# RWKV-7 stage of a hybrid trunk layer: score products that alternate heads, low-rank products on all 128 rows, small sums moved beside recurrence products

## The chip, the cores and the metric

The kernel runs on 1 core of one Trainium2 chip. The metric is the device time of one execution in microseconds (us). Before the change it is 2905.15 us, the median of 3 runs (2900.6 to 2907.33).

## What is computed

One layer of a streaming encoder over 4096 tokens of 1024 features: four mixers of 256 columns each (RWKV-7, pooling, mLSTM, retention), a gated embedding and an output projection with a layer norm. The change lies in the RWKV-7 mixer alone. Cut to what matters, with 4 heads of 64:

```python
z = z + (prev - z) * mu                       # token shift
r, k, v, wl, al = split(z)
decay = exp(-exp(-softplus(-(w0 + tanh(wl) @ w2)) - 0.5))   # low-rank, 64 inner columns
a = sigmoid(a0 + al @ a2)                                    # low-rank, 64 inner columns
kk = heads(k * k_k); kk = kk / max(norm(kk), 1e-12)
k = heads(k) * (1 + (a - 1) * k_a)
def step(state, ...):
    sa = state @ (-kk)
    state = state * w + sa * (kk * a) + v * k
    return state, state @ r
y = head_norm(scan(step)) * ln_w + ln_b + sum(r * k * r_k) * v
```

## The kernel before

The four mixers run one after another, and the output projection last. The RWKV stage (`_rwkv_out`) takes the tokens in 16 blocks of 256. The scan is done in chunks of 64 tokens: the scores of a chunk give a triangular matrix that is inverted, and a recurrence of four chunks carries the state through a block.

What a block goes through is cut into generators ("stages"), and the string `ORDER` says how they interleave. Each word is a stage, a lag in blocks and, after a slash, how many steps of it to run. `C` is one step of the recurrence `chain` of the block before last; there are 12 of them in a pass: per chunk `ry` (state and score products), `sa` (the inverse times the result), and `ds` with the second half of `ry` (state update and output). Between them stand dense projections (`la`, `k`, `r`, `g`, `v`, six products of 128x256 per step of one contraction tile, three for `la`) and small stages:

- `l`: the two low-rank products. Weights `LW` hold an upper and a lower part on 64 rows each. For both products and both column halves there is one matmul of `lah` over 128 rows, and one of `lal` (the lower part of the input) over the 64 rows that hold it.
- `n` and `bn`: sums over a head, 8 products of two columns each, with 64 output rows (128 contraction rows).
- `s0`, `s1`: transposes of `BK` into `st`, scaled into `ST` by VectorE. `p0`, `p1`: the scores of a pair of chunks, `gp`: for head `hh` of a pair (64 contraction rows each) four products, then four VectorE operations that scale and mask them into `g1`. `gp` has one PSUM buffer per head; `l`, `n`, `vt`, `st`, `gp` and `bn` share a pool of two.
- `inv`, `iv`, `pt`, `px`, `pu`, `py`: the inverse `X`, in part on VectorE (`iv`), through DRAM, and in 32-row products; `pt`, `px`, `pu`, `py` run one pass later. `sa` of the next pass reads `X`.

All these products go through `mm` (L273), which keeps them in the program's order on TensorE, so that the string is TensorE's order. The other engines' orders come from the tile scheduler. `soon()` raises the priority of the recurrence's and the inverse's operations there. float32 products are two records each in the trace.

```python
        mm = lambda *args, **kw: keep(nc.tensor.matmul(*args, **kw))
...
                    for p, hh, hv in heads:
                        mm(sa[bs, p, hv], X[bs, 4 * cc + 2 * hh + p], R[bs, p, hv], start=True, stop=True)
                    A.copy(out=SAV[cc][bs, e], in_=sa[bs].rearrange("p a v -> p (a v)"))
...
            for e in range(2):
                V.tensor_copy(out=X[top(e), :, 32:64], in_=t[top(e)])
            yield 0.6
```

Of the kernel before, what the change touches and what calls it, by code (L numbers as in the profile page):

```python
# [9 lines left out]
F32 = mybir.dt.float32  # L10
# [19 lines left out]
ORDER = "C la.0 C k.0/2 C k.0 C r.0/2 C l.0 r.0/3 C r.0/2 n.0 r.0/2 C vt.1 r.0 m.0 C g.0/4 C g.0 v.0/2 C s0.0 v.0/1 pt.1 C p0.0/1 v.0/1 px.1 C p0.0 v.0/2 bn.0 v.0 pu.1 s1.0 p1.0/1 py.1 p1.0 inv.0 iv.0"  # L30
# [12 lines left out]
class Trunk:  # L43
# [27 lines left out]
    def fetch(self, hi, lo, src, nm, eng):  # L71
        """load float32 data and split it exactly into hi + lo"""
# [14 lines left out]
    def weights(self, name, g0, w=G, pool=None, bufs=5, gates=False):  # L87
        """hi and lo parts of columns g0..g0+w of a weight matrix"""
# [16 lines left out]
    def lazy(self, *args, **kw):  # L105
        """a weight group that is loaded where it is first used"""
        box = []
        def get(split=False):
            if not box:
                w, parts = self.weights(*args, **kw)  # L110
                box.append(w)
                if split:
                    return parts
                list(parts)
            return box[0]
        return get

    def load_x(self, b, more=None, between=None):
        """the block's tokens in quarters of the contraction; three of eight come from the pool more"""
# [19 lines left out]
    def dense(self, jobs, nk=KT, apart=False):  # L139
        """out = lhsT.T @ rhs for each job; operands are (hi, lo) by contraction tile.  # L140
        The jobs share one bank unless apart and advance together, so one start flag clears it."""
# [7 lines left out]
    def dense_k(self, jobs):  # L149
        """the same in steps of one contraction tile, in this order on the engine"""  # L150
# [8 lines left out]
    def cols(self, z, w, x, n=2):  # L159
        """columns of one weight group on the partitions, tokens along the row"""  # L160
# [3 lines left out]
    def toks(self, jobs, nk=KT, apart=False):  # L164
        """tokens on the partitions: jobs of (out, weights, x, first token)"""
# [4 lines left out]
    def silu_gate(self, sg, z):  # L170
        """twice z * sigmoid(z)"""
# [13 lines left out]
    # ------------------------------------------------------------------ RWKV  # L185
# [6 lines left out]
    def _rwkv_out(self, es):  # L192
# [20 lines left out]
        # low-rank weights: decay rows (hi, lo), rate rows (lo, hi), against twice the upper part of their input  # L213
# [43 lines left out]
        def mixed(b, out, z, c0, n):  # L257
            """z + (previous token's z - z) * mu, by columns"""
# [11 lines left out]
        # what a block goes through, in pieces: generators that yield the time of the products they have issued  # L270
# [53 lines left out]
        def l(b):  # L324
            # low-rank decay and rate
            la = bl[b]["la"]
            lah = p1.tile([P, 2, TB], F32R, name=f"lah{b}", tag="E")
            lal = p1.tile([P, TB], F32R, name=f"lal{b}", tag="ta")
            lz = [wk.tile([P, 2, TB], F32, name=f"l{g}{b}", tag="wk") for g in range(2)]
            for g in range(2):  # L330
# [3 lines left out]
                V.tensor_tensor(out=lal[own], in0=la[own], in1=lah[own, g].bitcast(F32), op=ALU.subtract)  # L334
                for p in range(2):
                    mm(lz[g][:, p], LW[g][:, p], lah[:, g], start=(p == 0), stop=False, skip_group_check=True)
                    mm(lz[g][:, p], LW[g][own, p], lal[own], start=False, stop=True, skip_group_check=True)
# [20 lines left out]
        def n(b):  # L358
            # squared norm of the removal key, by tokens in the order of the rows of its products
# [11 lines left out]
            # rows (kappa, beta) of an even chunk, (beta, kappa) of an odd one  # L371
# [61 lines left out]
        def s_(b, cc):  # L433
            # token-major copies of (kappa, beta)
# [11 lines left out]
        def p_(b, cc):  # L446
            # scores of the chunk
            BK, rc, AR, g1 = (bl[b][x] for x in ("BK", "rc", "AR", "g1"))
            gp = [wk.tile([P, 2, 2, P], F32, name=f"gp{b}_{cc}_{hh}", tag="wk") for hh in range(2)]
            for hh in range(2):  # L450
                sl = slice(64 * hh, 64 * hh + 64)
                for p in range(2):
                    for e in range(2):
                        mm(gp[hh][:, p, e], BK[sl, p, cc, 2 * e:2 * e + 2].rearrange("p a t -> p (a t)"),
                           AR[cc][sl, p, 2 * e:2 * e + 2].rearrange("p a t -> p (a t)"), start=True, stop=True)
                for p in range(2):
# [5 lines left out]
                yield 0.87  # L462
# [37 lines left out]
        # inverse of I - N, N strictly upper in this layout  # L500
# [23 lines left out]
        def iv(b):  # L524
# [3 lines left out]
            with self.soon():  # L528
                # the four blocks of 4 on the diagonal, row by row from below
# [7 lines left out]
                # pairs of blocks: X12 = X11 (N12 X22), the inner product where N has zeros  # L537
# [25 lines left out]
        def pt(b):  # L563
            # pairs of 16 to blocks of 32: rows and columns of one block of 32, what N has in the pairs meets zeros
# [29 lines left out]
        def pu(b):  # L594
            # blocks of 32 to 64
# [23 lines left out]
        def chain(b):  # L619
            """the four chunks of a block, one after another; yields where their products wait"""  # L620
# [90 lines left out]
    def head_norm(self, pool, Y, eps, nm):  # L711
        """normalise each 64-wide head of Y [P, 2, 256] in place"""
# [18 lines left out]
    # ------------------------------------------------------------------ pooling  # L731
    def pooling(self, es):
# [12 lines left out]
        # the first products wait for these alone  # L745
# [79 lines left out]
    # ------------------------------------------------------------------ retention  # L825
# [133 lines left out]
    # ------------------------------------------------------------------ mLSTM  # L959
    def gates(self, cp, es0):  # L960
        """the stabiliser and the decays of every chunk of 128 tokens, rows (chunk, head)"""
# [69 lines left out]
    def _mlstm(self, es):  # L1031
# [12 lines left out]
        def operand(n):  # L1044
            """the right operand n of v, o and the gate; three of them leave room for a left operand each"""
# [19 lines left out]
        def dense(b):  # L1065
# [31 lines left out]
            # the halves of the block's tokens: rows of the contraction k0 .. k0 + 3, tokens of half c  # L1097
# [68 lines left out]
        def mix(b):  # L1166
# [25 lines left out]
            for c in range(2):  # L1192
# [4 lines left out]
                # decayed scores, transposed: rows are the keys  # L1197
# [22 lines left out]
                # carry of the memory  # L1220
# [16 lines left out]
                # h = num / max(|den|, exp(-m))  # L1237
# [448 lines left out]
```

## Time and profile before

| | before |
|---|---|
| median of 3 runs | 2905.15 us |
| profiled execution: span from first to last instruction | 2898.2 us |
| median less that span (what lies around it, and scatter) | 6.95 us |
| TensorE (PE) busy | 2773.1 us, 96% |
| VectorE (DVE) busy | 2270.0 us, 78% |
| ScalarE (ACT), GpSimd (POOL) busy | 34%, 40% |
| mean granted TensorE clock | 0.974 |

The profile gives no time of the profiled execution other than its span, so that the runs' median stands beside it. PE busy counts a matmul from its start to its end, and matmuls overlap: a stretch that is busy throughout may hold products that follow each other closely or slowly. What a group of products costs is therefore read from the start of its first product to the start of what comes next. The RWKV stage lies between about 1255 and 2190 us of the span.

### The profile page before, as it was taken

Reading aid. Unit: us, or ns where it says so; the run is one execution under the profiler, and the core shown is the slowest. Engines: PE = TensorE matmul, PEld = TensorE weight load, DVE = VectorE, ACT = ScalarE, POOL = GpSimd, SP = SyncE. Lnnn points to the kernel's source line nnn. Section 1 sums busy time; section 2 is a strip of 40 time slices with the busy share of each in tenths; the row PEclk is TensorE's granted clock in tenths of the full one; section 3 lists DMA queues with packets and bytes.
Section 4 is the critical chain, followed back from the end, with each engine's and each line's share of the span. In section 5 each row is a group of like instructions: output and inputs, shape, how many; then the busy total and the mean of one; then the engine's idle time right before and its main releaser. Section 6 shows DMA issues by size and latency. Waiting matters only on the chain.

```text
span 2898.2 us, 57364 instructions
## 1 busy us (share of the span) xinstructions
PE 2773.1 (96%) x21940; PEld 2466.1 (85%) x21940; DVE 2270.0 (78%) x5639; ACT 974.5 (34%) x2100; POOL 1156.9 (40%) x1231
## 2 busy tenths in 40 slices
PE   7899999999999999798999999999999999999997
PEld 7898888878999999688999999998998788777885
DVE  5657788887999999976777777778847566689997
ACT  3423223234433333333333333334423233432221
POOL 6654555553333333421232333223326111156665
PEclk9899999999999999888999999999999999999998
DMA  7743222223211111321111111112437444643441
GB/s 241 218 142 102 59 66 66 63 72 110 71 59 56 59 53 55 103 59 29 47 34 41 44 37 45 34 45 60 133 106 260 149 139 138 221 153 139 148 157 66
DMA packets 250499, 281.13 MB, mean 97 GB/s; under 512 B 69488, under 2 KB 166512, under 8 KB 250224
## 3 DMA queue, kind: packets, MB, share of 16 engines
q1 hardware_dynamic: 250224, 277.46, 30.5%
q8 instruction: 172, 2.82, 0.4%
q14 instruction: 103, 0.84, 0.1%
HBM read 209.69 MB, written 67.70 MB: 96 GB/s over the span
## 4 chain that ended last, share of the span: by engine, by line
PE 41%; DVE 10%; POOL 3%; DMA 2%; issue 2%; ACT 1%; SPq 0%; POOLq 0%; DVEq 0%; ACTq 0%
PE ry L273 3%; PE gp L273 2%; DVE ro L1578 2%; DVE ro L1557 1%; PE sa L273 1%; PE l L273 1%; PE zg L154 1%; DVE ro L1560 1%; PE zpl L147 1%; PE zpl L145 1%; PE zpl L146 1%; PE zg L155 1%; PE zg L156 1%; POOL ro L1561 1%; PE zpe L145 1%
## 5 line engine op out<-in xcount | busy, mean ns | idle before, releaser
L1336 ACT CAST Ah<-xr 128x512 fp32r<-128x512 f32 x189 | 117.0, 620 | 277.7 <-PE zrb L1372 58.7
L1337 DVE TENSOR_TENSOR Al<-xr,Ah 128x512 fp32r<-128x512 f32 x135 | 99.8, 739 | 76.5 <-ACT Ah L1336 75.7
L677 POOL TENSOR_TENSOR SAV<-SAV,bon 64x256 f32<-64x256 f32 x64 | 40.7, 636 | 283.9 <-PE ry L273 282.3
L85 DVE TENSOR_TENSOR xl<-rawx,xh 128x512 fp32r<-128x512 f32 x148 | 120.9, 821 | 39.8 <-ACT xh L84 38.9
L145 PE MATMUL zqk<-xh,wh_w_ml 128*128 128x256 f32 x512 | 149.1, 291 | 1.1 <-ACT xh L1078 1.1
L146 PE MATMUL zqk<-xl,wh_w_ml 128*128 128x256 f32 x512 | 149.1, 291 | 0.3 <-DVE xl L1079 0.3
L147 PE MATMUL zqk<-xh,wl_w_ml 128*128 128x256 f32 x512 | 149.2, 291 | 0.0
L84 ACT CAST xh<-rawx 128x512 fp32r<-128x512 f32 x148 | 91.6, 619 | 168.8 <-DMA rawx<-in_xT 72.3
L1337 POOL TENSOR_TENSOR Al<-xr,Ah 128x512 fp32r<-128x512 f32 x54 | 71.8, 1330 | 135.7 <-ACT Ah L1336 72.2
L1561 POOL TENSOR_TENSOR ro<-ro,ln_b 128x512 f32<-128x512 f32 x64 | 100.6, 1591 | 53.9 <-DVE ro L1560 53.9
L660 DVE SCALAR_TENSOR_TENSOR S<-ds,eC,Se 64x64 f32<-64x64 f32 x256 | 72.5, 283 | 53.4 <-PE ds L273 48.7
L866 POOL TENSOR_TENSOR rot<-rot,sw 128x256 f32<-128x256 f32 x64 | 69.4, 1085 | 94.2 <-DVE sw L865 88.5
L145 PEld LDWEIGHTS zqk<-xh,wh_w_ml 128*128 128x128 f32 x512 | 98.0, 191 | 3.6 <-ACT xh L1078 1.6
L147 PEld LDWEIGHTS zqk<-xh,wl_w_ml 128*128 128x128 f32 x512 | 98.1, 192 | 2.4
L146 PEld LDWEIGHTS zqk<-xl,wh_w_ml 128*128 128x128 f32 x512 | 98.2, 192 | 2.0 <-DVE xl L1079 0.8
L459 DVE SCALAR_TENSOR_TENSOR g<-gp,rc,c_rmask 128x128 f32<-128x128 f32 x256 | 72.1, 343 | 33.9 <-PE gp L273 32.8
L145 PE MATMUL zu<-xh,wh_w_pl 128*128 128x256 f32 x256 | 78.7, 308 | 14.7 <-ACT xh L84 8.9
L1356 POOL TENSOR_TENSOR xr<-xr,xr 128x512 f32<-128x512 f32 x27 | 35.5, 1316 | 141.8 <-DVE xr L1353 141.7
L146 PE MATMUL zu<-xl,wh_w_pl 128*128 128x256 f32 x256 | 78.2, 305 | 12.0 <-DVE xl L85 12.0
L1185 DVE SCALAR_TENSOR_TENSOR xc<-zc,c_convw,xc 128x256 f32<-128x256 f32 x192 | 86.2, 497 | 0.4
L273 PE MATMUL ry<-SAV,g 64*64 64x64 f32 (+1 forms) x1024 | 83.5, 223 | 0.0
L798 DVE SCALAR_TENSOR_TENSOR dp<-s,c_pinv,us 64x256 f32<-64x256 f32 (+1 forms) x64 | 44.5, 695 | 47.9 <-POOL s L784 41.7
(1120 smaller groups left out, 10675.9 us busy)
## 6 DMA issues: line engine op xcount, KB each, us to landing
rawx<-in_xT SPq DMA_DIRECT2D x148, 256.0 KB, 3.3
xr<-in_xT SPq DMA_DIRECT2D x108, 256.0 KB, 2.9
mr<-in_xT SPq DMA_DIRECT2D x64, 256.0 KB, 3.1
rp<-in_x SPq DMA_DIRECT2D x64, 256.0 KB, 3.1
s<-rp SPq DMA_DIRECT2D x64, 256.0 KB, 2.5
yo<-y SPq DMA_DIRECT2D x16, 1024.0 KB, 4.9
ro<-s SPq DMA_DIRECT2D x16, 1024.0 KB, 5.0
out<-ro SPq DMA_DIRECT2D x32, 512.0 KB, 2.6
```

The costliest lines, as they stand in the source:

```text
L84: nc.scalar.copy(out=hi, in_=raw)
L85: eng.tensor_tensor(out=lo, in0=raw, in1=hi.bitcast(F32), op=ALU.subtract)
L145: nc.tensor.matmul(out, lh(k), rh(k), start=(k == 0 and (apart or i == 0)), stop=False, skip_group_check=True)
L146: nc.tensor.matmul(out, lh(k), rl(k), start=False, stop=False, skip_group_check=True)
L147: nc.tensor.matmul(out, ll(k), rh(k), start=False, stop=(k == nk - 1), skip_group_check=True)
L273: mm = lambda *args, **kw: keep(nc.tensor.matmul(*args, **kw))
L459: V.scalar_tensor_tensor(out=g1[cc][:, hh, p, e], in0=gp[hh][:, p, e], scalar=rc[:, cc, e, i:i + 1], in1=msk[:, 64 * e:64 * e + P], op0=AL ...
L660: V.scalar_tensor_tensor(out=Sn[hv, p, hv], in0=ds[hv, p], scalar=eC[hv, p, c:c + 1], in1=Se[hv, p], op0=ALU.mult, op1=ALU.add)
L1185: V.scalar_tensor_tensor(out=xc[:, t], in0=zc[t // 2][:, t % 2, j:j + TB], scalar=cw[:, t, j:j + 1], in1=xc[:, t], op0=ALU.mult, op1=ALU.add)
L1336: self.nc.scalar.copy(out=hi, in_=src)
L1337: eng.tensor_tensor(out=lo, in0=src, in1=hi.bitcast(F32), op=ALU.subtract)
L1561: Q.tensor_tensor(out=rg, in0=rg, in1=ln["ln_b", g], op=ALU.add)
```

## The change

`ORDER` is written anew, the score products alternate the two heads, and the low-rank products all span 128 rows. The input's lower part `lal` gets a second copy with zeros in the other 64 rows (two GpSimd memsets per block). Docstrings and comments are emptied, which moves line numbers by up to 4; they are left out here.

```diff
-ORDER = "C la.0 C k.0/2 C k.0 C r.0/2 C l.0 r.0/3 C r.0/2 n.0 r.0/2 C vt.1 r.0 m.0 C g.0/4 C g.0 v.0/2 C s0.0 v.0/1 pt.1 C p0.0/1 v.0/1 px.1 C p0.0 v.0/2 bn.0 v.0 pu.1 s1.0 p1.0/1 py.1 p1.0 inv.0 iv.0"
+ORDER = "C la.0 C k.0/2 C k.0 C r.0/2 C l.0 r.0/3 C n.0 r.0/4 C vt.1 r.0 m.0 C g.0/4 C g.0 v.0/2 C s0.0 v.0/1 pt.1 C p0.0 v.0/2 px.1 C bn.0 v.0/1 s1.0 v.0/2 pu.1 v.0/1 p1.0 v.0 py.1 inv.0 iv.0"
...
-            lal = p1.tile([P, TB], F32R, name=f"lal{b}", tag="ta")
+            lal = p1.tile([P, 2, TB], F32R, name=f"lal{b}", tag="ta")
...
                 A.copy(out=lah[other, g], in_=la[own])
-                V.tensor_tensor(out=lal[own], in0=la[own], in1=lah[own, g].bitcast(F32), op=ALU.subtract)
+                Q.memset(lal[other, g].bitcast(F32), 0.0)
+                V.tensor_tensor(out=lal[own, g], in0=la[own], in1=lah[own, g].bitcast(F32), op=ALU.subtract)
+            for g in range(2):
                 for p in range(2):
                     mm(lz[g][:, p], LW[g][:, p], lah[:, g], start=(p == 0), stop=False, skip_group_check=True)
-                    mm(lz[g][:, p], LW[g][own, p], lal[own], start=False, stop=True, skip_group_check=True)
+                for p in range(2):
+                    mm(lz[g][:, p], LW[g][:, p], lal[:, g], start=False, stop=(p == 1), skip_group_check=True)
...
             gp = [wk.tile([P, 2, 2, P], F32, name=f"gp{b}_{cc}_{hh}", tag="wk") for hh in range(2)]
-            for hh in range(2):
-                sl = slice(64 * hh, 64 * hh + 64)
-                for p in range(2):
-                    for e in range(2):
+            for p in range(2):
+                for e in range(2):
+                    for hh in range(2):
+                        sl = slice(64 * hh, 64 * hh + 64)
                         mm(gp[hh][:, p, e], BK[sl, p, cc, 2 * e:2 * e + 2].rearrange("p a t -> p (a t)"),
                            AR[cc][sl, p, 2 * e:2 * e + 2].rearrange("p a t -> p (a t)"), start=True, stop=True)
+            for hh in range(2):
                 for p in range(2):
                     for e in range(2):
...
-                yield 0.87
+            yield 0.87
```

The order of instructions changes with it. Three places, all in the pass of block 7.

TensorE, from the inverse's product `px` on, before (`ds`, `ry`: recurrence; `gp_0_1`: scores of the second head; `z7v`: dense projection):

```order
L273 MATMUL px_19636<-X_19135,TD 32x16 x32
L273 MATMUL ds_3_19673<-SAV_1_18693,ST_1_17986 64x64 x4
L273 MATMUL ry_3_19557<-SAV_1_18693,g_1_17988 64x64 x4
L273 MATMUL gp_0_1_19621<-AR_0_19449,BK_19448 128x128 x4
L154 MATMUL z7v<-xh_4_19161,wh_w_rw_14376 128x256
```

The same place now:

```order
L273 MATMUL px_19666<-X_19149,TD 32x16 x32
L273 MATMUL ds_3_19703<-SAV_1_18707,ST_1_17998 64x64 x4
L273 MATMUL ry_3_19573<-SAV_1_18707,g_1_18000 64x64 x4
L273 MATMUL bn_19755<-rkw,rk_19479 64x2 x8
L154 MATMUL z7v<-xh_4_19175,wh_w_rw_14376 128x256
```

The sums `bn` follow the recurrence's products directly, and the second head's scores have gone up to the first head's. `n` is moved in the same way behind the second `ds` and `ry` of the pass.

VectorE, at the end of the pass, before (`g_1`: masked scores of the second pair of chunks; `X<-py`: the last part of the inverse; `v`, `Y`: other work):

```order
L459 SCALAR_TENSOR_TENSOR g_1_19468<-gp_1_0_19803,rc_14302,c_rmask 128x128 x4
L265 SCALAR_TENSOR_TENSOR v_19768<-z7v,c_prm,v_19768 128x255
L268 TENSOR_TENSOR v_19768<-v_19768,zf_19172 128x2
L726 TENSOR_TENSOR Y_19138<-Y_19138,rsr_19712 128x512
L617 COPY X_19135<-py_19813 32x8x32 x2
L459 SCALAR_TENSOR_TENSOR g_1_19468<-gp_1_1_19804,rc_14302,c_rmask 128x128 x4
```

The same place now:

```order
L463 SCALAR_TENSOR_TENSOR g_1_19484<-gp_1_0_19819,rc_14302,c_rmask 128x128 x4
L463 SCALAR_TENSOR_TENSOR g_1_19484<-gp_1_1_19820,rc_14302,c_rmask 128x128 x2
L265 SCALAR_TENSOR_TENSOR v_19790<-z7v,c_prm,v_19790 128x255
L268 TENSOR_TENSOR v_19790<-v_19790,zf_19186 128x2
L463 SCALAR_TENSOR_TENSOR g_1_19484<-gp_1_1_19820,rc_14302,c_rmask 128x128
L730 TENSOR_TENSOR Y_19152<-Y_19152,rsr_19742 128x512
L463 SCALAR_TENSOR_TENSOR g_1_19484<-gp_1_1_19820,rc_14302,c_rmask 128x128
L621 COPY X_19149<-py_19837 32x8x32 x2
```

The second head's four operations, which stood behind the copies into `X`, now stand ahead of them.

VectorE, in the middle of the pass, before (`Z_0`: transpose of `X` as it comes from DRAM; `S`: the recurrence's state; `BK`, `AR`: operands of the scores):

```order
L265 SCALAR_TENSOR_TENSOR r_19416<-z7r,c_prm,r_19416 128x255
L268 TENSOR_TENSOR r_19416<-r_19416,zf_19172 128x2
L402 TENSOR_TENSOR BK_19448<-ta_19332,tw_19331 128x2x128 x2
L408 TENSOR_TENSOR AR_0_19449<-r_19416,E_19340 128x2x2x64
L660 SCALAR_TENSOR_TENSOR S_14298<-ds_2_19500,eC_17864,Se_2_19505 64x64 x4
L567 STREAM_TRANSPOSE Z_0_19578<-X_19135 128x512
```

The same place now:

```order
L265 SCALAR_TENSOR_TENSOR r_19432<-z7r,c_prm,r_19432 128x255
L268 TENSOR_TENSOR r_19432<-r_19432,zf_19186 128x2
L571 STREAM_TRANSPOSE Z_0_19594<-X_19149 128x512
L405 TENSOR_TENSOR BK_19464<-ta_19348,tw_19347 128x2x128 x2
L411 TENSOR_TENSOR AR_0_19465<-r_19432,E_19356 128x2x2x64
L664 SCALAR_TENSOR_TENSOR S_14298<-ds_2_19516,eC_17876,Se_2_19521 64x64 x4
```

The transpose, which waits for a transfer, stands ahead of the operands and of the state update.

## Rows read from the trace of the kernel before

**Rows 1.** Busy time in a 55 us stretch of the RWKV stage, columns as named.

```profile
core 0: us, PE busy (x) PEld busy (x) DVE busy (x) ACT busy (x) POOL busy (x), PEclk, DMA share, GB/s
1475.00:1530.00 55.00, 55.00 (x677) 50.29 (x675) 41.93 (x131) 20.19 (x51) 17.88 (x27) 1.00 0.14 39
```

**Rows 2.** Timeline, PE: start, length, instruction. The low-rank products' first, and what follows.

```profile
1511.07 0.38 PE L273 MATMUL l<-lah,LW 128*128 128x256 f32 x1
...
1513.57 0.39 PE L154 MATMUL z5r<-xh,wh_w_rw 128*128 128x256 f32 x1
```

**Rows 3.** Timeline, PE: dense products before and behind the sums n.

```profile
1518.06 0.28 PE L155 MATMUL z5r<-xl,wh_w_rw 128*128 128x256 f32 x1
1518.18 0.28 PE L156 MATMUL z5r<-xh,wl_w_rw 128*128 128x256 f32 x1
1518.39 0.65 PE L273 MATMUL n<-ones,sq 128*64 128x2 f32 x16
1518.97 0.38 PE L154 MATMUL z5r<-xh,wh_w_rw 128*128 128x256 f32 x1
1519.20 0.28 PE L155 MATMUL z5r<-xl,wh_w_rw 128*128 128x256 f32 x1
```

**Rows 4.** Timeline, PE: scores to the next pass's sa, dense products left out.

```profile
1534.14 1.16 PE L273 MATMUL gp<-AR,BK 64*128 64x128 f32 x8
...
1536.13 0.73 PE L273 MATMUL px<-X,TD 32*32 32x16 f32 x64
1536.79 0.45 PE L273 MATMUL ds<-SAV,ST 128*64 128x64 f32 x8
...
1537.64 1.16 PE L273 MATMUL gp<-AR,BK 64*128 64x128 f32 x8
...
1544.85 0.69 PE L273 MATMUL py<-X,T 32*32 32x32 f32 x32
1545.47 1.16 PE L273 MATMUL gp<-AR,BK 64*128 64x128 f32 x8
1546.55 0.71 PE L273 MATMUL ry<-S,AR 128*128 128x128 f32 x4
...
1550.87 0.68 PE L273 MATMUL sa<-R,X 64*64 64x64 f32 x8
```

**Rows 5.** Timeline, PE: the retention stage's scores, whose heads alternate, and the next product.

```profile
504.91 0.71 PE L920 MATMUL sc<-qT,kT 64*128 64x128 f32 x8
505.56 0.50 PE L1372 MATMUL zrb<-rB6wlg,Ah 128*128 128x512 f32 x1
```

**Rows 6.** Single records' lengths in ns (min/median/max), by line: scores and sums.

```profile
L273 PE MATMUL gp<-AR,BK x512: 272/272/578, 1280.7 to 2062.8; 64*128 64x128 f32 x171
L273 PE MATMUL n<-ones,sq x256: 197/198/218, 1269.0 to 2030.4; 128*64 128x2 f32 x128
```

**Rows 7.** Timeline, DVE, same pass as rows 4: what leads up to the copies into X.

```profile
1535.34 1.13 DVE L459 SCALAR_TENSOR_TENSOR g<-gp,rc,c_rmask 128x128 f32<-128x128 f32 x4 [2.10 <-PE gp L273]
1536.89 0.69 DVE L85 TENSOR_TENSOR xl<-rawx,xh 128x512 fp32r<-128x512 f32 x1 [0.43 <-ACT xh L84]
...
1544.14 0.68 DVE L440 TENSOR_TENSOR ST<-st,rc 128x512 f32<-128x512 f32 x1
...
1547.43 0.84 DVE L617 COPY X<-py 32x256 f32<-32x256 f32 x2
```

**Rows 8.** PE: low-rank products' start; windows (span, busy, granted clock, DMA share, GB/s).

```profile
1458.91 0.38 PE L273 MATMUL l<-lah,LW 128*128 128x256 f32 x1
...
1460.00:1462.50 2.50, 2.50 (x10) 0.79 0.00 0
1462.50:1465.00 2.50, 2.50 (x14) 0.53 0.00 0
```

**Rows 9.** Waits in the RWKV stage: total us, times, longest us.

```profile
PE pt L273 <- DVE Z L567: 7.3, 1, 7.3
...
DVE Z L567 <- DMA X<-xd: 5.9, 2, 5.4
```

## The prediction

> **What bounds the kernel now.** I read the page's forty slices first: PE is at 9 tenths nearly throughout. The windows of the RWKV stage say the same more sharply: in a 55 us stretch PE is busy for all 55.00 us, DVE for 41.93 [rows 1]. PE is the bound there, but "busy" does not mean that products follow closely, so I went to the timeline of PE and measured from start to start. Dense products of one shape start every 0.12 us (1518.06, 1518.18). Where the shape changes the distance grows: 0.21 from the last dense one to the first `n`, and 0.23 from the first dense one behind `n` to the second [rows 3]. So a change of shape costs about 0.09 on the side that is left and 0.11 on the side that is entered. A pass of the stage has 46 such changes (counted along the built order), the changed one 31. That is what the change works on. Last I looked at DVE's timeline, for what would hold PE once PE is quicker.
>
> **Low-rank products.** Eight products alternate two shapes, 128 and 64 contraction rows. From the first to the dense product behind them it is 1513.57 - 1511.07 = 2.50 us, 0.31 each [rows 2], and that dense product pays 0.11 more for re-entry [rows 3]. Now all eight have the dense products' shape: 8 x 0.12, and 0.11 for entering behind `sa`: 1.07. Saved: 2.50 + 0.11 - 1.07 = 1.54 us per block. That the lower part now multiplies 64 rows of zeros costs nothing by itself: the columns that stream are the same 256. The two memsets stand in POOL's queue behind the product `rk` and before the state's `Se`; POOL is busy 17.88 of 55 us [rows 1], and they run half a pass before `l` needs them. I count nothing; without that cover two operations of a few tenths each would delay `Se`, and through it the state update.
>
> **Sums n.** Now: 0.21 + 0.58 + 0.23 = 1.02 us from the dense product before to the second one behind, where two dense steps would be 0.24, so `n` costs 0.78 [rows 3]. Behind `ds` and `ry`, which have its shape, it pays no change of its own: 16 records at (0.65 - 0.20) / 15 = 0.03 us [rows 3, 6], 0.48. Saved: 0.30.
>
> **From the scores to the next pass.** From the first `gp` to the next pass's `ry` it is 1546.55 - 1534.14 = 12.41 us [rows 4]. I set this stretch together anew. A group of scores of one head has 8 records; they span 1.16, one lasts 0.27, so they start every 0.127 us, and the group takes 1.08 with its tail of 0.19 [rows 4, 6]. What 16 records with alternating heads take no row of this stage shows, but the retention stage has the same product (64x128, moving 128 columns) with alternating heads: 8 records span 0.71, hence one every (0.71 - 0.27) / 7 = 0.063 us, and the group takes 0.65, its tail 0.21 [rows 5, 6]. The bounds are 0.063 and 0.127 per record; I take 0.063, since that row differs in nothing that I can see. A group of 16 is then 15 x 0.063 + 0.21 = 1.15 us, in place of two at 1.08. The stretch becomes, in its new order: scores 1.15; 12 dense products 12 x 0.12 + 0.11 + 0.09 = 1.64; `px` 0.66; `ds` and `ry` 0.85 [rows 4] and `bn` 0.48 as `n`; 6 dense products 0.83; `st`, of the dense shape, 4 x 0.12 = 0.48; 12 dense products and leaving 1.53; `pu` as `py` 0.62; scores 1.15; `py` 0.62. Sum 10.01, saved 2.40.
>
> For the same product the Trainium skill ("TensorE: Matmul & The Clock Gate", LDWEIGHTS) puts the load of a 128-column weight at about 107 ns. If loads ran singly, 16 records would take 1.71 and not 0.95, and a block would lose up to 1.5 us of the saving; by the row they do not, since eight such loads fit into a 0.71 us group.
>
> **What DVE gives back.** In this stretch DVE runs almost without a pause from the first masked score at 1535.34 to the end of the copies into `X` at 1548.27: 12.93 us with one pause of 0.43 [rows 7]. The next pass's `sa` reads `X`; it starts at 1550.87, 2.6 us later [rows 4]. With the change PE reaches `sa` 2.40 us earlier, 14.33 us behind the first `gp` and not 16.73. DVE, however, now has all sixteen masked scores of the pass ahead of the copies, where the last four stood behind them (second place of the order above): four more, 1.1 us, less the pause, which closes: 13.6 us. It starts 1.2 us behind `gp` as now, so `X` is ready at 14.8 and `sa` waits about 0.5 us. The PSUM slots press at the same place: the second head's scores need the slot that the scaling `ST` (1544.14) frees, which is now barely before them; that wait falls inside the 0.5. So 1.93 of the 2.40 stay. Per block: 1.54 + 0.30 + 1.93 = 3.77 us. The bounds are 4.24 (no wait) and about 2.8 (another microsecond of such waits).
>
> **Sum.** Blocks 2 to 15 have the recurrence beside them: 14 x 3.77 = 52.8. In the first two passes `n` and `bn` stand between dense products as before, and the one long wait of the stage, 7.3 us of `pt` for the transpose [rows 9], is there: what comes earlier is waited for. I count 2 us each for their scores, 4, with 0 and 8 as ends. The clock comes on top. In the windows of 2.5 us, in five passes with the recurrence the granted clock falls to its lower level, 1.2 GHz, each time 1 to 5 us behind the start of the low-rank products. For one of them: 2.5 x 0.21 + 2.5 x 0.47 = 1.7 us lost [rows 8]. Before it PE ran `sa` and those eight products with their nine changes of shape. The eight become as dense as the projections, behind which the clock stays up, and I expect these falls to go: 7 of 8.5 us, ends 0 and 8.5. Together 64 us. The profiled span of 2898.2 becomes 2834; with the 6.95 us by which the median stands above that span, 2841. Behind the stage the same work follows, only earlier.
>
> **Rivals.** (a) *The heads do not overlap:* records stay at 0.127 us, 0.95 more per group, 1.9 per block; then DVE's run is no longer in the way, and a block saves 1.84 + 0.5 = 2.3: 14 x 2.3 + 2 + 7 = 42, 2863. For it: the `gp` rows themselves, and weight loads one by one, as above, would lead halfway. Against it: rows 5. (b) *DVE becomes the bound in that stretch:* its order is fixed, and each wait of PE for a PSUM slot or for `X` returns as a later start; 2.8 per block and the clock's falls stay, since new pauses take the place of the changes of shape: 14 x 2.8 + 4 = 43, 2862. For it: 0.43 us of pause in 12.93 [rows 7]. Against: DVE has 13 us of 55 free elsewhere [rows 1]. (c) *Slower:* on DVE the transpose for `pt` now stands ahead of the operands `BK`, `AR` and the state update `S`, and it waits for a transfer. Before, that wait came twice, 5.9 us in all, the longer 5.4 [rows 9]. If the transfer came late in each block, `S` and through it `ry` would be late each time. It decides from 4 us per block on; at 5.4 in 14 blocks it takes 76 us against 53 + 4 gained with the clock as before: 2924. Against it: the waits were few, and the inverse's operations on DVE are moved by little. (d) *Nothing comes of it:* the built order has the new shapes next to each other, so only a price of shape changes that does not depend on the neighbours would do that; rows 2 and 3 speak against it. 2905.
>
> **Chances.** Forecast 0.74, (a) 0.09, (b) 0.12, (c) 0.03, (d) 0.02. The likeliest case runs from 2832 (no wait for DVE, every fall of the clock gone) to 2852 (waits, clock as before); below it lies the scatter of runs, 4.5 us down to the lowest. The range takes in (a) and (b): 2828 to 2865. A measurement here can tell 0.2%, 5.8 us, from no change. Faster 0.94, same 0.03 (d and a weak (b) with the edges against it), slower 0.03.
>
> **What would show it.** Right: the eight `l` records start every 0.12 us; 16 `gp` records span about 1.2 us; `n` and `bn` directly behind `ry`; passes shorter by some 3.8 us; granted clock full behind `l`; a short wait of `sa` for the copies into `X`. Wrong: `gp` records every 0.127 us; long waits of PE on DVE's `ST`, `X` or `S`; a transpose `Z` that waits for the transfer in every pass; new falls of the clock elsewhere.

## The result, and the profile after

| | before | changed |
|---|---|---|
| median | 2903.87 us of 4 runs (2900.6 to 2907.33) | 2851.37 us of 4 runs (2850.36 to 2852.05) |
| ratio of the runs | | 0.9823, 95% interval 0.9808 to 0.9838 |
| span of the profiled execution | 2898.2 us | 2848.6 us |
| TensorE (PE) busy | 2773.1 us | 2703.9 us |
| VectorE (DVE) busy | 2270.0 us | 2266.1 us |
| mean granted TensorE clock | 0.974 | 0.974 |

The change takes off 52 us where 64 were forecast; the forecast time was 2841 us. One more run of the kernel before was made beside the changed one, so its median is 2903.87 here. In lines of `kernel.py`, the changed kernel is 4 higher than the kernel before in this stage; `mm` is still L273.

The window of one steady pass of the changed kernel answers to [rows 1]: span, then busy time of PE, weight loads, DVE, ACT and POOL, then granted clock, DMA share and GB/s.

```profile
1540.00:1587.00 47.00, 46.61 (x639) 43.69 (x637) 39.64 (x126) 19.14 (x50) 14.03 (x25) 1.00 0.17 44
```

PE is no longer busy throughout: 0.39 us of the pass are waits. The timeline of PE in that pass, for [rows 2 to 4] (start, length, instruction, what the idle time ahead waited for):

```profile
1540.03 0.51 PE L273 MATMUL l<-lah,LW 128*128 128x256 f32 x2
...
1541.10 0.28 PE L154 MATMUL z6r<-xh,wh_w_rw 128*128 128x256 f32 x1
...
1543.63 0.63 PE L273 MATMUL ry<-SAV,g 128*64 128x64 f32 x8
1544.10 0.63 PE L273 MATMUL n<-ones,sq 128*64 128x2 f32 x16
1544.66 0.39 PE L154 MATMUL z6r<-xh,wh_w_rw 128*128 128x256 f32 x1
...
1561.28 1.16 PE L273 MATMUL gp<-AR,BK 64*128 64x128 f32 x16
1562.37 0.39 PE L154 MATMUL z6v<-xh,wh_w_rw 128*128 128x256 f32 x1
...
1568.93 0.69 PE L273 MATMUL pu<-Z,g 32*32 32x32 f32 x32 [0.17 <-DVE mvr L724]
...
1576.06 0.65 PE L273 MATMUL sa<-R,X 64*64 64x64 f32 x8 [0.23 <-DVE X L621]
```

The low-rank products take 1541.10 - 1540.03 = 1.07 us up to the next dense product, as forecast, and that product is short (0.28), so it pays nothing for entering. `n` follows `ry` and costs 0.56. Sixteen scores span what eight spanned: 1.16 us. From the first `gp` to the next pass's `sa` it is 1576.06 - 1561.28 = 14.78 us, its two waits included; before it was 16.73. From pass to pass, `l` starts every 46.86 us, against 50.66 in a pass of the kernel before without a fall of the clock: 3.8 us, forecast 3.77.

The waits of the stage (total us, times, longest), for [rows 9]; the last row is one of DVE for a transfer:

```profile
PE pt L273 <- DVE Z L571: 8.3, 2, 8.0
PE n L273 <- ACT sq L366: 5.7, 3, 4.7
PE sa L273 <- DVE X L621: 2.4, 11, 0.2
PE pu L273 <- DVE mvr L724: 1.9, 12, 0.2
PE gp L273 <- DVE ST L443: 1.4, 1, 1.4
...
DVE Z L571 <- DMA X<-xd: 21.9, 16, 6.0
```

Each pass has two short waits for DVE, 0.4 us together. The one wait for `ST` stands alone, in pass 13. Passes are counted here by the block whose `l` they begin with, from 0; pass 13 is called the thirteenth in the expectations. Granted clock of PE in windows of 2.5 us, behind the low-rank products of a steady pass (they start at 1586.90) and in pass 13, for [rows 8]:

```profile
1588.50:1591.00 2.50, 2.50 (x34) 1.00 0.00 0
...
1897.50:1900.00 2.50, 1.08 (x14) 1.00 0.18 45
1900.00:1902.50 2.50, 2.50 (x44) 0.62 0.18 66
1902.50:1905.00 2.50, 2.50 (x15) 0.50 0.32 104
1905.00:1907.50 2.50, 2.50 (x14) 0.51 0.22 53
```

Behind `l` the clock stays at 2.4 GHz. In passes 2 to 12 it falls nowhere; in pass 13 it lies at 1.2 GHz for nearly 7 us, and PE had waited 1.42 us just before. The timelines there: PE in pass 13, and then DVE, with its row for `ST` one pass earlier ahead of its rows in pass 13:

```profile
1897.35 0.48 PE L273 MATMUL gp<-AR,BK 64*128 64x128 f32 x2
1899.25 1.16 PE L273 MATMUL gp<-AR,BK 64*128 64x128 f32 x14 [1.42 <-DVE ST L443]
```

```profile
1850.18 0.69 DVE L443 TENSOR_TENSOR ST<-st,rc 128x512 f32<-128x512 f32 x1
...
1897.18 0.68 DVE L729 TENSOR_TENSOR Y<-Y,mvr 128x512 f32<-128x512 f32 x1
1897.79 0.69 DVE L85 TENSOR_TENSOR xl<-rawx,xh 128x512 fp32r<-128x512 f32 x1
1898.51 0.69 DVE L443 TENSOR_TENSOR ST<-st,rc 128x512 f32<-128x512 f32 x1
```

In passes 2 to 14 only this one has `ST` behind the norm's `Y` and a split `xl` (the subtraction that leaves the lower part of the next block's tokens) in DVE's built order. Relative to `l` of its block, `ST` is 1898.51 - 1868.07 = 30.4 us late in place of 1850.18 - 1821.20 = 29.0.

**Where the gain stands, by the starts of `l`.** At block 13 the changed kernel is ahead by 1920.87 - 1868.07 = 52.8 us; forecast were 4 for the first passes, 11 x 3.77 and 7 for the clock, 52.5. At block 14 it is ahead by 52.5 (pass 13 gave nothing, 4.1 less than its share), at block 15 by 2022.61 - 1966.05 = 56.6, at the end by 49.6. Pass 14 gained 4.1, and from the start of block 15's `l` to the end 7.0 are lost. So the forecast fits until block 13, and what is missing lies in pass 13 and behind the start of block 15. For that last part, windows of both kernels counted from the start of block 15 (span, PE busy, granted clock, DMA share, GB/s), the kernel before first:

```profile
2022.60:2070.00 47.40, 46.47 (x577) 0.96 0.42 122
2070.00:2120.00 50.00, 50.00 (x599) 1.00 0.40 121
2120.00:2320.00 200.00, 189.27 (x1214) 0.97 0.55 181
```

```profile
1966.00:2013.40 47.40, 42.19 (x571) 0.96 0.40 111
2013.40:2063.40 50.00, 50.00 (x539) 0.97 0.41 127
2063.40:2263.40 200.00, 185.77 (x1258) 0.98 0.55 178
```

PE idles 5.2 us in place of 0.9 beside the last block, where DVE is busy 29.3 of 30 us (1960 to 1990) with the recurrence and the splits of the gated embedding's weights at once, and 14.2 in place of 10.7 in the 200 us behind (2063.40 to 2263.40). DVE is as full beside the last block of the kernel before, 29.0 of 30 us (2016 to 2046), but there PE comes at its slower pace. What PE waits for in these 200 us, and below it one wait of ACT:

```profile
PE zplb L1377 <- POOL Al L1341: 4.9, 1, 4.9
PE zpl L145 <- ACT ep L1442: 4.5, 2, 3.1
PE zpla L1375 <- ACT Ah L1340: 3.4, 1, 3.4
...
ACT Ah L1340 <- DMA xr<-in_xT: 12.5, 1, 12.5
```

In the kernel before, the windows shown first have waits for `ep` (2.8), `pl` (2.3) and for the transfer of `yo` (5.1). The gated embedding starts earlier, and its operands `Ah` and `Al` don't come earlier by as much: `Ah` has its own wait for a transfer, the last row, which was 8.1 us in the kernel before. That an earlier start is the reason is not shown: with the scores alone (first experiment below), whose gated embedding starts later than before, PE idles 14.4 us in the same 200 us.

### The profile page after: what moved, and what is told of

Same layout as the page of the kernel before. It is cut to its first block, busy times and chain, and to the rows that moved or that the text cites. A ratio compares the mean times of both kernels' runs of the same rounds, so it can differ in the third digit from the quotient of the medians.

```text
span 2848.6 us, 57425 instructions
## 1 busy us (share of the span) xinstructions
PE 2703.9 (95%) x21940; PEld 2422.4 (85%) x21940; DVE 2266.1 (80%) x5639; ACT 971.6 (34%) x2100; POOL 1142.9 (40%) x1263
## 4 chain that ended last, share of the span: by engine, by line
PE 32%; DVE 14%; DMA 4%; POOL 3%; issue 3%; ACT 1%; SPq 0%; POOLq 0%; DVEq 0%; ACTq 0%
PE ry L273 3%; DVE ro L1582 2%; DVE ro L1561 1%; PE sa L273 1%; DVE ro L1564 1%; PE zg L154 1%; POOL ro L1565 1%; PE zg L155 1%; PE zg L156 1%; DVE so L1556 1%; PE zpe L145 1%; PE ds L273 1%; PE zpe L147 1%; DVE g L463 1%; PE zpe L146 1%
## 5 line engine op out<-in xcount | busy, mean ns | idle before, releaser
L273 PE MATMUL ry<-SAV,g 64*64 64x64 f32 (+1 forms) x1024 | 84.0, 224 | 0.0
```

## Experiments: the three parts alone

**The scores alone.** The kernel before with the new `p_` and nothing else.

```diff
-            for hh in range(2):
-                for p in range(2):
-                    for e in range(2):
+            for p in range(2):
+                for e in range(2):
+                    for hh in range(2):
...
-                yield 0.87
+            yield 0.87
```

> The kernel before, with the scores of the two heads alternating and nothing else of the change. My theory: 16 records of gp span about 1.16 us as in the changed kernel, so two groups of 8 at 1.08 become one of 1.15: 1.0 us per chunk, 2.0 per block, 28 us in 14 blocks, and PE still waits next to nothing for the copies into X, which had 2.6 us to spare. The granted clock still falls to its lower level behind the low-rank products, since those are as before. About 2875 us. Rival: the alternation pays only together with the new order (the masked scores of both heads now come at once on DVE, and what PE gains it waits for): less than 1 us per block, 2890 or more, with waits of PE on DVE in each pass.

Measured: 2939.73 us, ratio 1.014, interval 1.0125 to 1.0155: 40 us slower. My theory was wrong in sign; the rival, that the alternation pays only together with the new order, came true. Every pass takes 54.6 us. PE, and windows of PE's granted clock, in one of them:

```profile
1495.67 0.69 PE L273 MATMUL pu<-Z,g 32*32 32x32 f32 x32 [0.24 <-DVE Z L599]
...
1496.88 0.49 PE L273 MATMUL gp<-AR,BK 64*128 64x128 f32 x2
1498.23 1.16 PE L273 MATMUL gp<-AR,BK 64*128 64x128 f32 x14 [0.86 <-DVE ST L440]
```

```profile
1500.00:1502.50 2.50, 2.50 (x16) 0.52 0.26 91
1502.50:1505.00 2.50, 2.50 (x14) 0.50 0.23 56
1505.00:1507.50 2.50, 2.50 (x16) 0.62 0.21 19
...
1520.00:1522.50 2.50, 2.50 (x12) 0.61 0.23 26
```

The second record pair of the second chunk's scores belongs to the other head, and takes the PSUM slot that `ST` has to free first. In the old order of the stages the transposes `st` stand directly ahead of these scores, so PE waits for DVE each time (`ST` ends at 1498.18 in this pass). Behind that wait the clock lies at 1.2 GHz for 7 us, and again behind `l` (1518.08). Per pass: 2.0 saved, 1.1 waited, 2.5 x (0.48 + 0.50 + 0.38) = 3.4 lost behind the wait, some 1.7 behind `l`, in us: 50.66 - 2.0 + 1.1 + 5.1 = 54.9, measured 54.6. The wait of 1.1 us costs less than the clock that follows it.

**The low-rank products alone.** The kernel before with the memsets, `lal` on 128 rows and the grouped loop.

> The kernel before, with the low-rank products on 128 rows and grouped, and nothing else of the change. My theory: 1.5 us per block, 21 to 22 us in 14 blocks, and the five falls of the granted clock behind these products go as well, 7 us more: about 2875 us, passes of 49.1 us, and the clock full in passes 2 to 12. Rival: the falls of the clock come from the scores and the sums before the low-rank products, or from none of them: they stay, one in about two passes, and the time is 2882 us.

Measured: 2872.24 us, ratio 0.9902, interval 0.9885 to 0.9918. Passes of 49.13 us: 50.66 - 49.13 = 1.53, forecast 1.54. Behind the low-rank products (here at 1556.54) the clock is full, as everywhere between block 2 and the end of the stage's passes:

```profile
1558.50:1561.00 2.50, 2.50 (x30) 1.00 0.00 0
```

So the falls in the kernel before hung on these eight products; scores and sums are as they were. The next kernel, which keeps the eight as they were, keeps the falls behind them.

**The order alone.** The kernel before with the new `ORDER`.

> The kernel before, with the new order of the stages alone: n behind ds and ry, bn behind the next ds and ry, both heads' scores of a chunk next to each other. My theory: 0.30 us for n, as much for bn, and some 0.4 for the changes of shape saved between the scores: 1.0 us per block, 14 us; the clock falls as before behind the low-rank products: about 2889 us. Rival: without quicker scores the order gains nothing, because the products that the recurrence waits for come later by what stands ahead of them now: 2900 or more.

Measured: 2883.6 us, ratio 0.995, interval 0.9933 to 0.9967. It saves 16 us although the clock falls more often, ten times in the passes, eight of them behind `l`: the granted share that is missing sums to 30 us over the stage (1250 to 2200), before to 22. At equal clock it saves nearer 24. The scores of one chunk, head behind head:

```profile
1731.52 1.71 PE L273 MATMUL gp<-AR,BK 64*128 64x128 f32 x16
1733.16 0.39 PE L154 MATMUL z9v<-xh,wh_w_rw 128*128 128x256 f32 x1
```

Next to each other the two groups take 1.64 us, not twice 1.09 [rows 4]. That is 0.54 per chunk which I had put down to the alternation; the alternation itself adds 1.64 - 1.09 = 0.55 more. Passes without a fall of the clock take 48.80 us, 1.86 less than such a pass of the kernel before: 2 x 0.54 for the scores, the rest for `n`, `bn` and the changes of shape around them. 14 x 1.86 = 26, less the 8 us of clock 18, against 16 measured.

The three parts alone give +40, -27 and -16 us, 3 us less in sum; together they give 52 less. The alternation loses without the order, because `st` has to move away from the scores that need its slot.

**Two steps of one part.** The changed kernel with the lower part back on 64 rows, two products at a time.

```diff
-                    mm(lz[g][:, p], LW[g][:, p], lal[:, g], start=False, stop=(p == 1), skip_group_check=True)
+                    mm(lz[g][:, p], LW[g][own, p], lal[own], start=False, stop=(p == 1), skip_group_check=True)
```

> The changed kernel, with the lower parts of the low-rank products back on 64 rows, two products in a row at a time, and without the memsets. It separates the two halves of that step: the number of shape changes (four more per block here than in the changed kernel, eight more in the kernel before) from the rows themselves. My theory: each change costs about 0.2 us, so 0.8 us per block, 11 us in 14 blocks: about 2862 us, and some of the falls of the clock return (up to 2870). Rival one: being next to each other is what counts and the rows do not: within 3 us of the changed kernel, 2851. Rival two: the 64-row products are slow in themselves, and nearly the whole step is given back: 1.5 us per block, 2873 or more.

Measured: 2860.45 us, ratio 0.9859, interval 0.9843 to 0.9874. Passes of 47.60 us, 0.74 more than in the changed kernel: four more changes of shape at 0.185 us each. 14 x 0.74 = 10.4, and the two ratios differ by 0.0036 of 2900, 10.4. No fall of the clock behind these products returns.

```profile
1535.79 0.50 PE L273 MATMUL l<-lah,LW 128*128 128x256 f32 x2
...
1537.50 0.39 PE L154 MATMUL z6r<-xh,wh_w_rw 128*128 128x256 f32 x1
```

It is now 1.71 us up to the dense product, which pays for entry again. This kernel has the same four 64-row products as the kernel before and half of its extra changes of shape, and it pays half: 0.74 for four changes, 1.53 for eight. The number of changes is the price; the rows are not.

## Experiments: the wait for ST, and the hand-over

**The transposes earlier.** The kernel with the scores alone, and `s1` moved up: in the built order by six dense products and `pu`, not by the twelve of the expectation.

```diff
-... bn.0 v.0 pu.1 s1.0 p1.0/1 py.1 p1.0 inv.0 iv.0"
+... bn.0 v.0/1 s1.0 v.0 pu.1 p1.0/1 py.1 p1.0 inv.0 iv.0"
```

> The kernel with the alternating scores alone, which took 40 us more than the kernel before: in each pass PE waits 0.83 us in the second chunk's scores for DVE's scaling ST, whose PSUM slot the second head's scores take, and behind that wait and behind the low-rank products the granted clock lies at its lower level (77 us of clock lost in the stage, against 22 in the kernel before). Here the transposes s1, which ST follows, are issued 12 dense products earlier, and nothing else is moved. My theory: the wait for that one slot is the whole cause. It goes, with it the fall behind it; 2.0 us per block stay as saved: 2875 us, passes of about 48.7 us, with falls of the clock behind the low-rank products as in the kernel before. Rival one: DVE is the bound in that stretch whatever the order; ST comes no earlier, or another wait takes its place: 2915 us or more. Rival two: the slower clock comes from the alternating scores themselves, two row groups at once: no wait, but the clock still falls in each pass: 2910 us.

Measured: 2932.06 us, ratio 1.0112, interval 1.0099 to 1.0126. Rival one came true. PE waits 25.4 us for `ST`, in every second pass up to 4.1 us at once; passes without it take 49.1 us. DVE in a bad pass:

```profile
1762.56 0.68 DVE L726 TENSOR_TENSOR Y<-Y,mvr 128x512 f32<-128x512 f32 x1
...
1764.78 0.69 DVE L727 TENSOR_TENSOR Y<-Y,rsr 128x512 f32<-128x512 f32 x1 [0.93 <-POOL rsr L724]
...
1766.95 0.69 DVE L440 TENSOR_TENSOR ST<-st,rc 128x512 f32<-128x512 f32 x1
```

`st` is done at 1761.82, so `ST` could have run some 4 us earlier (an estimate from these rows); the order built for DVE puts it behind four operations of the norm, one of which waits for POOL. Where the transposes stand on PE does not settle when `ST` runs: its place in DVE's order does, as in pass 13 of the changed kernel.

**Less work on DVE, by the splits.** The changed kernel with two of four splits of the next block's tokens on POOL (`load_x` takes the engine for the quarters from the third on).

> The changed kernel, with half of the splits of the next block's tokens (the subtraction that leaves xl) on POOL and not on DVE, two of four per block: 1.3 us less for DVE in the stretch in which it runs without a pause up to the copies into X. My theory: the short waits of PE for X and for the sums' mvr, 0.4 us per pass, go, and in pass 13 ST is no longer late (1.4 us of wait and 3.4 us of clock lost behind it): 5 to 9 us less than the changed kernel, 2843 to 2846. Rival: POOL's longer operations (1.22 against 0.68 us) delay the norm's power rsr and the state's Se, and a wait of PE for those takes their place: 2851 or more.

Measured: 2849.31 us, ratio 0.9831, interval 0.9818 to 0.9845: no difference that can be told. Pass 13's wait and fall are gone, but each pass takes 47.14 us, 0.28 more. PE, and DVE's row for the copies:

```profile
1580.76 0.65 PE L273 MATMUL sa<-R,X 64*64 64x64 f32 x8 [0.66 <-ACT la L264]
```

```profile
1579.77 0.84 DVE L621 COPY X<-py 32x256 f32<-32x256 f32 x2
```

The wait is put down to ACT, whose `la` `sa` does not read; the copies into `X`, which it does read, end at 1580.61, 0.15 before it. The expectation of the run with both reliefs, below, says that they moved behind the masked scores. That is not so: they stand behind all of them in the changed kernel too. What is new is that DVE waits 0.54 us for POOL's `rsr` in the norm ahead of the last masked scores, which run later for it, and that the norm's next operation `Y` (L684) has moved ahead of the copies. That is the rival's kind of delay.

**The small weight earlier.** The changed kernel with `wple()` called ahead of the last quarter of the gate's weight, and so ahead of `embedded(b)` as well.

> The changed kernel, with the small weight of the gated embedding loaded ahead of the last quarter of the gate's weight, not behind it. It tests where the gain is lost at the hand-over behind the stage: there PE waits 2.1 us for that weight, and the granted clock falls behind the wait (3.3 us lost). My theory: both go, 5 us less than the changed kernel, about 2846. Rival: the load of the quarter is late instead and PE waits for that, or DVE and ACT, full with the splits of these weights, make it late all the same: 2851, no change.

Measured: 2849.67 us, ratio 0.9829, interval 0.9816 to 0.9842: no difference. The wait for the weight is gone, but `sa` waits 2.1 us for `X` (up to 2014.6) in its place. The clock is at 1.2 GHz from 2007.5 to 2021, longer than in the changed kernel (2010 to 2017); PE had waited 1.1 us up to 2005.1 for `Z`. The window of ten of these us (the third number from the end is the granted clock):

```profile
2010.00:2020.00 10.00, 7.42 (x57) 6.47 (x52) 8.52 (x20) 4.67 (x9) 3.19 (x4) 0.50 0.47 130
```

**The copies into X on ACT.** The changed kernel with one line changed.

```diff
-                V.tensor_copy(out=X[top(e), :, 32:64], in_=t[top(e)])
+                A.copy(out=X[top(e), :, 32:64], in_=t[top(e)])
```

> The changed kernel, with the two copies of py into X (0.84 us a pass) on ACT and not on DVE. ACT is busy 19 of 47 us in a pass and DVE 40. In the order that is built, the thirteenth pass has ST ahead of the norm on DVE again, as the other passes have. My theory: sa no longer waits for X (0.2 us in each pass), the wait for ST in pass 13 goes (1.4 us) and with it the fall of the clock that follows it (3.4 us at half): passes of 46.6 us, and in all about 7 us less than the changed kernel, 2844. Rival: X comes late from ACT, whose queue has the copies T, R and xh ahead, and sa waits more; or what pass 13 gains is waited for at the hand-over to the gated embedding, where DVE is full: 2851, no change.

Measured: 2840.77 us, ratio 0.9796, interval 0.9782 to 0.981. Passes of 46.60 us, pass 13 included; the wait for `X` is gone and the clock is full there:

```profile
1576.09 0.67 PE L273 MATMUL sa<-R,X 64*64 64x64 f32 x8
```

```profile
1900.00:1902.50 2.50, 2.50 (x23) 1.00 0.29 94
```

12 x 0.26 + 4.4 for pass 13 = 7.5 us; by the ratios it is 0.0027 of 2900, 7.8, or 0.0030, 8.7, against the second run of the changed kernel (0.9826, below). The two forecast effects, the wait for `X` and pass 13, are both there.

**Both reliefs in the passes.** The copies on ACT and the splits on POOL.

> Both reliefs of DVE at once: the copies into X on ACT, and half of the splits of the next block's tokens on POOL. With the splits alone on POOL, each pass was 47.14 us in place of 46.86, because the copies into X had moved behind the masked scores on DVE and sa waited 0.65 us for them. My theory: that wait goes with the copies off DVE, passes of 46.5 us, no wait for ST anywhere, about 2840 us. Rival: another operation of DVE or POOL takes the place of the copies as what comes last, passes of 46.9 us or more: 2848 to 2852.

Measured: 2841.69 us, ratio 0.9799, interval 0.9785 to 0.9813. Passes of 46.41 us, as forecast, but two longer ones (47.1 and 49.2) between blocks 5 and 7 in the profiled execution, and the time is that of the copies alone. In the first of the two PE waits 0.5 us for `ST`, in the second 1.7 for ACT's copy `SAV` and 0.5 for `S`; the forecast had no wait for `ST` anywhere. Ahead of the wait for `SAV`, DVE had waited 3.8 us for the transfer of `nt`, and `SAV` stands on ACT behind `k` and `sq`, which wait for DVE's `k`.

**The gate's weight.** The changed kernel with two of four splits of each quarter of the gate's weight on POOL, in place of one.

> The changed kernel, with one more of the four splits of each quarter of the gate's weight on POOL and not on DVE: 2.8 us less for DVE in the last three blocks of the stage, where it is busy 29 of 30 us (1960 to 1990). My theory: the last three blocks gain less than the others because DVE is full there with these splits: with fewer of them PE's waits of 0.3 to 1 us for sq, R, S and Z shrink, and 2 to 4 us come back: 2848. Rival: POOL, whose operation takes 1.3 to 2.5 us, delays the state's Se and the gates' products, and nothing is gained: 2851 or more.

Measured: 2847.72 us, ratio 0.9819, interval 0.9804 to 0.9834. By the medians it is 3.6 us less than the changed kernel, by the ratios 1.2: it fits the theory at most in size, and runs differ by as much.

**The changed kernel again, and the best version.** The copies on ACT and the gate's splits on POOL together.

> The changed kernel itself, once more, for a direct comparison on one chip with the two reliefs of DVE: 2851 us, passes of 46.86 us, in the thirteenth pass 1.4 us of wait for ST and a fall of the granted clock behind it. If these come again at the same place, they belong to the built order and not to the single run that was profiled.

> The changed kernel with both reliefs of DVE that gave something alone: the copies of py into X on ACT (10.6 us less than the changed kernel) and one more split of the gate's weights on POOL (3.6 us less, hardly more than runs differ). My theory: they act at different places, the first in each pass and in pass 13, the second at the hand-over; both together about 2837 us. Rival: the second acts only by where it puts other operations on DVE, and beside the first it gives nothing: 2841.

Measured on one chip: the changed kernel 2849.06 us, ratio 0.9826, interval 0.9811 to 0.9842, with the same wait of 1.4 us in pass 13 and the same fall behind it (1902 to 1910); the version with both 2836.82 us, ratio 0.979, interval 0.9773 to 0.9806. The intervals do not meet: this version beats both kernels, the changed one by 12 us. Against the copies alone the intervals overlap, so that the second part's gain (4 us by the medians, 1.7 by the ratios) stays unproven.

## Why the prediction was right and where it failed

The direction, the mechanism and the size per pass hold. By its own steps:

- *Low-rank products, 1.54 us per block:* 1.53 measured with them alone. The memsets cost nothing that shows.
- *Sums n, 0.30:* `n` took 0.78 and now takes 0.56; `ds` and `ry` paid their changes of shape already. It saves 0.22.
- *Scores, 0.063 us per record:* (1.16 - 0.27) / 15 = 0.059. Rival (a) falls. Half of this saving is owed to the two groups standing together, half to the alternation, which the prediction did not part. The Trainium skill ("TensorE: Matmul & The Clock Gate", LDWEIGHTS) estimates a load by its columns, 128 / 1.2, about 107 ns. The trace agrees with that as the distance between loads of one row group (eight of one head span 0.96 us, the first row below, and one record lasts 0.19: 0.11 from start to start). It does not hold as a price per load where two row groups alternate: sixteen take 0.97 us from first start to last end (second row), for the loads of the two heads run side by side, as the row of the retention stage said.

```profile
1534.14 0.96 PEld L273 LDWEIGHTS gp<-AR,BK 64*128 64x128 f32 x8
...
1561.28 0.97 PEld L273 LDWEIGHTS gp<-AR,BK 64*128 64x128 f32 x16
```

- *What DVE gives back, 0.5:* 0.4, in the waits of `sa` for `X` and of `pu` for `mvr`. From the scores to `sa` 16.73 - 14.78 = 1.95 us are saved, forecast 1.93. The press for the slot of `ST` was seen, but as something that "falls inside the 0.5". It is the sharpest edge of the change: it costs 1.1 us per pass, and 3.4 us of clock behind the wait, when the order does not make room for it, and it is what the one lost pass is owed to.
- *Clock, 7:* no falls behind `l` in eleven passes, where five in the kernel before cost 8.5; that the low-rank products are the reason is shown by the kernel with them alone. Over the whole execution the clock gave back less: the mean is 0.974 in both. Of the 8.5 us pass 13 takes back 3.4, the hand-over 1.7, and stretches outside the stage 1.4.
- *Rival (c)*: its mechanism is there, and with it one of the prediction's signs of being wrong: `Z` waits for its transfer in each pass, mostly 1.0 to 1.4 us, 21.9 in all in place of 5.9. But PE's waits for `S` are 0.4 us in all; DVE had the time.

The step that failed is the sum: "14 x 3.77" and "Behind the stage the same work follows, only earlier". The passes of blocks 2 to 12 paid as forecast. The last three blocks were to gain 11 us and gave back 3: the pass of block 13 gained nothing, that of block 14 its 4.1, and from the start of block 15 on 7.0 were lost.

In pass 13 the built order of DVE differs, which is rival (b) for one pass: 1.4 us of wait and 3.4 of clock. It is shown by the second run of the changed kernel, in which it returns at its place, and by the copies on ACT, in which another order takes it away with its cost.

From the start of block 15's `l` the changed kernel needs 882.6 us where the kernel before needs 875.6, with 8.8 us more of idle PE. Of these, 4.3 are beside the last block, where DVE has the recurrence and the next stage's weights to split, 3.5 in the gated embedding, where `ep`, `Ah` and `Al` come late, 1.0 later. It belongs to this kernel and not to one execution: its second run needs 881.4. To come early is not what costs: the kernel with the low-rank products alone is there 23 us earlier than the kernel before and needs 874.3. What DVE has to do there is the likely cause: with the copies on ACT it is 878.8, with the gate's splits on POOL 877.6, and with both 875.1, as short as before the change. That is one profile each, and the other kernels here, some of them later than the kernel before, lie between 877 and 884, so that the cause stays likely and not shown; taking one wait away there can make another, as the small weight did. What holds `Ah` and `Al` was not tried: the wait for `Al` is there with the copies on ACT alone, 6.5 us, and not with the copies and the gate's splits together.

The time came nearer than the span, and that is luck. The span was forecast at 2834 us and is 2848.6, 14.6 more; the time was forecast at 2841 and is 2851.4, 10 more. The 6.95 us that the prediction added to the span are 2.8 now. Each run of the changed kernel takes 1.8 us more than its own span, so, if the kernel before does the same, the execution profiled before lay some 5 us below the median that stood beside it (an estimate).

## What to carry to other kernels

Price changes of shape on TensorE one by one, from start to start in the timeline, and put products of one shape next to each other; here a change costs 0.19 us, and that price held with eight changes taken away and with four. When products are brought together they need their buffers at the same time: look first at who frees them, and at that operation's place in the other engine's built order, pass by pass, because one pass in sixteen may be built otherwise. Part of a stage's gain can be lost at the seam to the next one: compare the two kernels from there to the end, and see which engine is full there already.

## What was not expected of the hardware

- Waits of PE of 0.24 and 0.86 us, close together in each pass, were followed by some 7 us at 1.2 GHz in each pass, 3.4 us lost; the 1.4 us in pass 13 likewise. At the hand-over the clock fell towards the end of the wait of 2.1 us for the small weight. The two waits of 0.2 us in each pass of the changed kernel were followed by none. It is not the wait's length alone: in the kernel with the splits on POOL, PE waits 1.2 us for `T` up to 2008.6, and the clock is 1.00 in the windows from 2000 to 2020; with both reliefs in the passes it is 1.00 from 1524 to 1600, with a wait of 1.7 us for `SAV` in between.
- Eight products that alternate two shapes, with PE busy throughout, were followed by the lower clock in five of the passes of blocks 2 to 15; with two visits to the other shape in place of four, in none. What decides which passes it hits is not shown.
- Two groups of products on different rows, one behind the other and not alternating, already overlap: they take 1.64 us in place of 2.18.
